# A two-block network on one core: more tokens by fetched rows in the first expert layer, fetches paced by eight, held lists, later modulation loads

## The chip, the cores and the metric

The kernel runs on one core of a Trainium2 chip. Its engines are TensorE (PE: matmuls and transposes), VectorE (DVE), ScalarE (ACT), GpSimd (POOL) and SyncE (SP), each with its own in-order queue of instructions; 16 DMA engines move data between HBM and the on-chip memory (SBUF). The metric is device time in microseconds of one execution. The kernel before took 2840.39 us, the median of three runs (2839.59 to 2842.22).

## The reference

A sequence of 256 tokens of width 1024, fp32, goes through two blocks. The part that matters here is the first block: two layers, each a mixer followed by an expert layer (`peer_ffn`); the mixer is an mLSTM in the first and a stick-breaking attention in the second. Before each half the input is normalised and modulated, `h * (1 + scale) + shift`, and after it gated; shift, scale and gate are six vectors of 1024 per layer, each the product of one conditioning vector with a 1024 x 1024 matrix (4 MB). The attention has two more such vectors for its shared keys and values.

```
def peer_ffn(h, w_q, sub_keys, peer_u, peer_v):   # per block of 128 tokens
    q = (xb @ w_q) as (128, 8 heads, 2, 128)
    s = q . sub_keys                              # (128, 8, 2, 128 keys)
    s_top, i_top = top_k(s, 16)
    cand = the 16 x 16 sums of both halves; g_top, pos = top_k(cand, 16)
    expert = 128 * i_first + i_second             # of 16384 experts
    act = gelu(u[expert] . xb);  out = sum softmax(g_top) * act * v[expert]
```

So each token uses 8 x 16 = 128 experts of 16384, and each expert has one row of 4 KB in a table u and one in a table v. The second block (two feed-forward pairs, an MLA and a forget-gate attention, a gated projection) is not touched.

## The kernel before

All stages run one after the other (`run`): mLSTM, expert layer 0 (`peer(0)`), attention (`stick`), expert layer 1 (`peer(1)`), then the second block. Weights stream through a ring of four 8 KB-per-partition tiles (`raw`, 1.05 MB each), loaded by SyncE's queue. A tool traces the program in order, places each engine's instructions by a simulated timeline, and may so move an instruction ahead of others of its engine; `issue_after(x)` forbids that it moves ahead of x on that engine.

**An expert layer does its tokens in two ways.** The first `TSL[l]` tokens (80 in layer 0, 96 in layer 1) are done by fetched rows: for one (token, expert) pair per partition, GpSimd's indirect DMA (`get`, L1392) fetches 128 rows of u (a 128x1024 tile), VectorE multiplies them with the token and sums (`up`, L1399), and later 128 rows of v are added, weighted, to an accumulator (`down`, L1416). That makes `TSL` fetches for u and as many for v. The other tokens are done densely: all 16384 experts' u against them (`u_phase`, L1443: 64 tiles of 1.05 MB, 16 matmuls each, with as many columns as there are dense tokens), gelu, times a matrix G of gates that is built from one-hot matrices (`g_phase`: VectorE builds them, 16 matmuls per 8 tokens, L1477), and times all of v (`v_phase`, L1494: 64 tiles).

**Order in an expert layer.** First the query projection `w_q`, with the scores and top-16 lists woven in. A list (`top16`, L1589 to L1593) is a maximum-of-8, a replacement, a second maximum-of-8 and two index searches on VectorE; each block of 128 tokens has 16 of them (`tops`), and then a routing step (`route`). Block 0 holds all tokens done by rows. Its lists and routing lead to `scatter`: expert numbers `ex` (L1335) and gates are spread over partitions by TensorE (L1343), masked and reduced on VectorE (L1347, L1349) into `sidx` and `sg`. The lists of block 1 only feed the one-hot matrices of dense tokens, but VectorE does them as soon as their scores exist. Then `par` weaves generators, in the order of the trace: twelve U tiles with the routing; twenty more with the rest of it, a part of the fetches `f` and of `extra`; 32 U tiles of the second group beside G of the first, 32 V tiles beside G of the second, 30 V tiles alone, each with a part of `f` and `extra`. The X tiles of the second U group lie in the memory that routing used. `extra` loads the modulation matrices that come next, a 128x1024 row tile at a time, by GpSimd's queue (`ada_acc`, L479): 48 tiles in layer 0, 8 in layer 1. They share six row buffers with the fetches (`row`).

**Pacing.** Every `PACE` fetches, `get` has TensorE transpose `PACE` columns of `sidx` (L1387), held behind the matmul traced last (`last_mm`), and ScalarE casts them to integers (`ix`, L1389, three buffers); GpSimd's fetches wait for that. So TensorE's position in its queue of tiles sets when a group of fetches may start.

**The attention's start.** `stick` normalises x, projects q (4 weight tiles), k and v (8), does 8 attention steps without weights, and the output projection (4). In `units`, after each weight tile once a credit is used up, one step of the modulation `ada` is taken: a 1.05 MB tile by SyncE's queue into the same ring, and two multiply-adds on VectorE (L497, L499). Eight such steps are taken there; they give shift and scale of the coming expert layer, used when `peer_open(1)` prepares its input after the attention steps. `bg_credit` starts at -2 * 2048, and each tile adds 2048.

Of the kernel before, what the change touches and what calls it, by code (L numbers as in the profile page):

```python
# [17 lines left out]
OP = mybir.AluOpType  # L18
AX = mybir.AxisListType
# [5 lines left out]
EPS = 1e-6  # L25
BIG = 1e30
GC = 64
TSL = (80, 96)
PACE = 4
GSC = 16384.0  # L30
QW = S + 2
TB = 8
# [65 lines left out]
def _units(l):  # L98

    return (0, 64), (64, TSL[l] - 64)  # L100

# [14 lines left out]
class Kern:  # L116
# [709 lines left out]
    def stick(self, ada):  # L826
        nc, I = self.nc, self.I
        m = self.mod[1]
        self.bg, self.bg_every, self.bg_credit = it.islice(ada, 8), 2048, -2 * 2048
        with self.tc.tile_pool(name="sky", bufs=1, reuse_waits="tile") as py, ExitStack() as inner:  # L830
            h2 = [py.tile([P, NK, S], F32R, name=f"hk{i}") for i in range(2)]
            pl = inner.enter_context(self.tc.tile_pool(name="sk", bufs=1, reuse_waits="tile"))
# [390 lines left out]
    def peer_open(self, l):  # L1223
# [4 lines left out]
        self.pr = self.pctx.enter_context(self.tc.tile_pool(name="pr", bufs=1, side="right", reuse_waits="tile"))  # L1228
        flat = self.pr.tile([P, GC * (S - TSL[l])], F32R, tag="X", name=f"late_{l}")
        n = NK * QW  # L1230
# [7 lines left out]
    def peer(self, l, extra=None):  # L1238


        nc, I = self.nc, self.I
        m = self.mod[l]
        TS, TD, UNITS = TSL[l], S - TSL[l], _units(l)
        NG = sum(n for _, n in UNITS)
        with ExitStack() as ctx:
# [12 lines left out]
            rp = rctx.enter_context(self.tc.tile_pool(name="rt", bufs=1, reuse_waits="tile"))  # L1258
            s_sb = [rp.tile([P, 16, P], F32, name=f"s_sb{i}_{l}") for i in range(2)]
# [38 lines left out]
            tv = [rp.tile([P, 16, 16], F32, name=f"tv{tb}_{l}") for tb in range(2)]  # L1298
            ti = [rp.tile([P, 16, 16], U32, name=f"ti{tb}_{l}") for tb in range(2)]
            ready = [], []  # L1300

            def tops(tb, n):
                for _ in range(min(n, len(ready[tb]))):
                    c = ready[tb].pop(0)
                    self.top16(rp, s_sb[tb][:, c, :], tv[tb][:, c, :], ti[tb][:, c, :])
            for c0 in range(0, 16, 4):
                pss = [self.ps("acc"), self.ps("acc")]
                for c in range(c0, c0 + 4):
                    hi, lo = next(us)
                    tops(0, 2)  # L1310
                    if c >= 2:
                        next(norm, None)
                    pq = self.ps()
                    self.lin_s(qT, hi, lo, P, pq[:, 0:QW])
                    qs = rp.tile([P, S], F32, tag="qs", bufs=2, name=f"qs_{l}_{c}")
                    sc = self.small(1, "qsh")
                    nc.scalar.copy(sc, pq[:, S:S + 1])
                    nc.vector.scalar_tensor_tensor(qs, rms, sc, pq[:, 0:S], OP.mult, OP.add)
                    for tb in range(2):
                        nc.tensor.matmul(pss[tb][:, (c - c0) * P:(c - c0 + 1) * P], qs[:, tb * P:(tb + 1) * P],  # L1320
                                         keys[:, c % 2, :], start=True, stop=True)
                for tb in range(2):
                    nc.scalar.activation(s_sb[tb][:, c0:c0 + 4, :], pss[tb].rearrange("p (a b) -> p a b", a=4), AF.Copy,
                                         scale=rs[tb])
                for r in ready:
                    r.extend(range(c0, c0 + 4))
# [4 lines left out]
            def scatter():  # L1331

                g, s0, s1 = chosen[0]
                e = rp.tile([P, P], F32, name=f"ex_{l}")
                nc.vector.scalar_tensor_tensor(e, s0, float(P), s1, OP.mult, OP.add)  # L1335
                if l:
                    nc.vector.tensor_scalar(e, e, float(l * P * P), None, OP.add)
                for i, (src, dst) in enumerate(((e, sidx), (g, sg))):
                    ps = self.ps()
                    o = 0  # L1340
                    for u, (t0, n) in enumerate(UNITS):
                        r = P // n
                        nc.tensor.matmul(ps[:, u * P:(u + 1) * P], spread[:, u, :], src, start=True, stop=True)  # L1343
                        tmp = rp.tile([P, P], F32, tag="r_sp", bufs=2, name=f"sp{i}{u}_{l}")
                        mk = smask[:, 0:r] if u == 0 else smask[:, 4:4 + r]
                        t3 = tmp.rearrange("p (k r) -> p k r", r=r)
                        nc.vector.tensor_mul(t3, ps[:, u * P:(u + 1) * P].rearrange("p (k r) -> p k r", r=r),  # L1347
                                             mk[:, None, :].to_broadcast([P, n, r]))
                        nc.vector.tensor_reduce(dst[:, o:o + n], t3, AX.X, OP.add)  # L1349
                        o += n  # L1350

            def route():
                while ready[0]:
                    tops(0, 2)
                    yield
                chosen[0] = yield from self.route(0, tv[0], ti[0], rp, pool)
                scatter()
                yield
                while ready[1]:
                    tops(1, 2)  # L1360
                    yield
                r1 = self.route(1, tv[1], ti[1], rp, pool)
                for _ in range(5):
                    next(r1)
                    yield
                self.routed(0, chosen[0], idx, TS)
                chosen[1] = yield from r1

            def fetched():
# [10 lines left out]
                def get(src, col):  # L1380

                    i = next(nth)
                    self.uid += 1
                    if i % PACE == 0:
                        ps = self.ps()
                        with self.tc.issue_after(self.last_mm.ins):
                            nc.tensor.matmul(ps[:, 0:PACE], self.ident, sidx[:, col:col + PACE], start=True, stop=True)  # L1387
                        held["ix"] = pool.tile([P, PACE], I32, tag="ix", bufs=3, name=f"ix_{self.uid}")
                        nc.scalar.copy(held["ix"], ps[:, 0:PACE])  # L1389
                    k = i % PACE  # L1390
                    row = self.row()
# [463 lines left out]
```

## Time and profile before

| what | value |
| --- | --- |
| median of 3 runs | 2840.39 us (2839.59 to 2842.22) |
| profiled execution | 2841.97 us |
| its span, first to last instruction | 2839.8 us |
| PE / PEld / DVE / ACT / POOL busy | 97 / 90 / 68 / 33 / 16% |
| mean granted TensorE clock | 0.986 |
| HBM read | 743.76 MB, 262 GB/s over the span |
| indirect fetches | 176 of u, 176 of v (80 + 96 each) |

How to read it: busy time is the union of an engine's instructions in the span; fp32 matmuls are recorded as two, so a dense tile of 16 matmuls shows as x32. DMA share is the mean busy share of 16 engines and can pass 1.0 where packets of two queues overlap. In the span, layer 0's first U matmul is at 238, its stage ends at about 907; layer 1's first is at 1125, and it ends at about 1745.

### The profile page before, as it was taken

To read this page: it belongs to the slowest core of one execution; us is meant where nothing else is said; L and a number is where in the kernel's file an instruction comes from. 1 tells how busy PE (TensorE), PEld (TensorE's weight loads), DVE (VectorE), ACT (ScalarE), POOL (GpSimd) and SP (SyncE) were. 2 spreads that over 40 slices of the span, in tenths; PEclk is the share of its full clock that TensorE was granted. 3 is DMA by queue.
4 is the path that set the end of the run, shared out by engine and by line. 5 is a ranking of instruction groups with operands and counts; after the bars stand their busy time and mean duration, and the time that the engine had idled before them with its cause. 6 is when DMAs were issued, how large, how long until landed. Compare 5 with 4: busy or idle time off the path is not lost.

```text
span 2839.8 us, 47705 instructions
## 1 busy us (share of the span) xinstructions
PE 2740.8 (97%) x19226; PEld 2544.7 (90%) x19226; DVE 1938.5 (68%) x4021; ACT 929.6 (33%) x1730; POOL 450.9 (16%) x445
## 2 busy tenths in 40 slices
PE   7999999999998999999999998999999999999999
PEld 4789989999998779999999987998799989877997
DVE  6778756767645978857777545667766666676665
ACT  4752111100000654111100002446654554456544
POOL 0000332333432000133344431000000000000000
PEclk9999999999999999999999999999999999999999
DMA  7655998999998634799999996554245555452553
GB/s 294 226 179 174 364 372 331 389 359 373 396 407 333 227 118 142 289 401 415 408 408 405 409 409 258 193 186 153 94 169 188 182 179 190 153 175 93 193 191 110
DMA packets 155580, 747.90 MB, mean 263 GB/s; under 512 B 15696, under 2 KB 17360, under 8 KB 111840
## 3 DMA queue, kind: packets, MB, share of 16 engines
q1 hardware_dynamic: 93984, 527.93, 49.9%
q0 software_dynamic: 58752, 213.94, 19.4%
q8 instruction: 151, 2.47, 0.4%
q10 hardware_dynamic: 2624, 3.00, 0.3%
q14 instruction: 69, 0.57, 0.1%
HBM read 743.76 MB, written 1.05 MB: 262 GB/s over the span
## 4 chain that ended last, share of the span: by engine, by line
PE 85%; DMA 7%; DVE 5%; ACT 2%; issue 1%; POOL 0%; SPq 0%; DVEq 0%; ACTq 0%; POOLq 0%
PE ps_acc L1494 17%; PE ps_mm L1443 17%; PE ps_mm L277 7%; PE ps_mm L279 7%; PE ps_mm L278 7%; DMA raw<-in_peer_v_dram 4%; PE ps_acc L244 4%; PE ps_acc L243 4%; PE ps_acc L245 4%; PE ps_acc L1149 3%; PE ps_acc L1151 3%; PE ps_acc L1150 3%; PE ps_mm L1477 1%; DMA raw<-in_ada_w_dram 1%; DVE wlo L229 1%
## 5 line engine op out<-in xcount | busy, mean ns | idle before, releaser
L229 DVE TENSOR_TENSOR wlo<-raw,whi 128x1024 fp32r<-128x1024 f32 (+1 forms) x440 | 532.6, 1214 | 243.4 <-ACT whi L228 232.7
L228 ACT CAST whi<-raw 128x1024 fp32r<-128x1024 f32 (+1 forms) x440 | 456.2, 1042 | 512.2 <-PE ps_mm L278 241.9
L1494 PE MATMUL ps_acc<-X,raw 128*128 128x176 f32 (+1 forms) x4096 | 608.0, 309 | 11.0 <-DMA raw<-in_peer_v_dram 10.8
L1443 PE MATMUL ps_mm<-hT,raw 128*128 128x176 f32 (+1 forms) x4096 | 604.6, 308 | 2.4 <-ACT jT L1673 2.4
L1494 PEld LDWEIGHTS ps_acc<-X,raw 128*128 128x128 f32 x4096 | 587.0, 191 | 16.2 <-DMA raw<-in_peer_v_dram 16.1
L1443 PEld LDWEIGHTS ps_mm<-hT,raw 128*128 128x128 f32 x4096 | 588.6, 191 | 3.4 <-ACT jT L1673 2.6
L277 PE MATMUL ps_mm<-xhi,whi 128*128 128x256 f32 (+1 forms) x1488 | 418.3, 283 | 7.4 <-ACT xhi L332 5.1
L278 PE MATMUL ps_mm<-xlo,whi 128*128 128x256 f32 (+1 forms) x1488 | 418.2, 282 | 3.3 <-DVE xlo L321 3.0
L279 PE MATMUL ps_mm<-xhi,wlo 128*128 128x256 f32 (+1 forms) x1488 | 417.9, 281 | 0.0
L1416 DVE SCALAR_TENSOR_TENSOR sacc<-row,dots,sacc 128x1024 f32<-128x1024 f32 x172 | 220.7, 1283 | 117.2 <-DMA row<-in_peer_v_dram,ix 116.2
L1399 DVE SCALAR_TENSOR_TENSOR row<-row,hn 128x1024 f32<-128x1024 f32 x176 | 213.1, 1224 | 114.7 <-DMA row<-in_peer_un_dram,ix 114.3
L277 PEld LDWEIGHTS ps_mm<-xhi,whi 128*128 128x128 f32 (+1 forms) x1488 | 279.6, 189 | 11.9 <-ACT xhi L332 5.3
L278 PEld LDWEIGHTS ps_mm<-xlo,whi 128*128 128x128 f32 (+1 forms) x1488 | 280.0, 188 | 7.3 <-DVE xlo L321 3.5
L279 PEld LDWEIGHTS ps_mm<-xhi,wlo 128*128 128x128 f32 (+1 forms) x1488 | 281.2, 189 | 0.5 <-DVE wlo L229 0.3
L1392 POOL DMA_INDIRECT row<-in_peer_un_dram,ix x176 | 209.9, 1192 | 446.7 <-ACT ix L1389 156.1
L1392 POOL DMA_INDIRECT row<-in_peer_v_dram,ix x176 | 197.2, 1120 | 340.2 <-ACT ix L1389 177.5
L1445 ACT ACTIVATE X<-ps_mm 128x352 f32<-128x352 f32 (+1 forms) x128 | 57.6, 450 | 495.5 <-PE ps_mm L1443 495.5
L1389 ACT CAST ix<-ps_mm 128x4 int32<-128x4 f32 x88 | 14.2, 161 | 511.8 <-PE ps_mm L1387 440.8
L1483 DVE SCALAR_TENSOR_TENSOR X<-ps_mm,X 128x128 f32<-128x128 f32 (+1 forms) x210 | 66.1, 365 | 125.2 <-PE ps_mm L1477 122.0
L1149 PE MATMUL ps_acc<-whi,ah 128*128 128x512 f32 x352 | 139.4, 396 | 0.0
L1151 PE MATMUL ps_acc<-whi,al 128*128 128x512 f32 x352 | 137.6, 392 | 0.0
L1150 PE MATMUL ps_acc<-wlo,ah 128*128 128x512 f32 x352 | 137.0, 389 | 0.0
(467 smaller groups left out, 3795.1 us busy)
## 6 DMA issues: line engine op xcount, KB each, us to landing
raw<-in_ffn_dram SPq DMA_DIRECT2D x132, 1024.0 KB, 4.8
raw<-in_peer_u_dram SPq DMA_DIRECT2D x128, 1024.0 KB, 7.9
raw<-in_peer_v_dram SPq DMA_DIRECT2D x128, 1024.0 KB, 11.3
raw<-in_ada_w_dram SPq DMA_DIRECT2D x28, 1024.0 KB, 5.4
row<-in_ada_w_dram POOLq DMA_DIRECT2D x40, 512.0 KB, 10.9
raw<-in_peer_wq_dram SPq DMA_DIRECT2D x16, 1024.0 KB, 4.8
raw<-in_fox_in_dram SPq DMA_DIRECT2D x12, 1024.0 KB, 5.1
raw<-in_ma_vo_dram SPq DMA_DIRECT2D x8, 1024.0 KB, 5.6
```

The costliest lines, as they stand in the source:

```text
L228: nc.scalar.copy(hi[:, 0:u], raw)
L229: nc.vector.tensor_sub(lo[:, 0:u], raw, hi[:, 0:u])
L277: nc.tensor.matmul(o, wh, xh[:, k, :], start=(k == 0), stop=False)
L278: nc.tensor.matmul(o, wh, xl[:, k, :], start=False, stop=False)
L279: self.last_mm = nc.tensor.matmul(o, wl, xh[:, k, :], start=False, stop=(k == NK - 1))
L1149: nc.tensor.matmul(o, ah[:, t], wh[:, n], start=(c == 0), stop=False)
L1150: nc.tensor.matmul(o, ah[:, t], wl[:, n], start=False, stop=False)
L1151: nc.tensor.matmul(o, al[:, t], wh[:, n], start=False, stop=(c == FFC - 1))
L1392: nc.gpsimd.indirect_dma_start(row, None, src, bass.IndirectOffsetOnAxis(held["ix"][:, k:k + 1], 0))
L1416: nc.vector.scalar_tensor_tensor(sacc[u], row, w, sacc[u], OP.mult, OP.add)
L1443: self.last_mm = nc.tensor.matmul(ps[:, i * TD:(i + 1) * TD], raw[:, o:o + P], hT[:, k, TS:S], start=(k == 0), stop=(k == NK - 1))
L1494: self.last_mm = nc.tensor.matmul(o, w, xs[:, 0, :], start=(first and c % 2 == 0), stop=last, skip_group_check=True)
```

## The change

The first layer does 96 tokens by rows (160 densely, 16 fewer), with two units of 64 and 32 tokens as the second layer has them. An index matmul and cast serve eight fetches. The top-16 lists of block 1 may not be placed ahead of the last reduction of `scatter`, in both layers. In the attention stage the first modulation step comes two weight tiles later.

```
-TSL = (80, 96)
-PACE = 4
+TSL = (96, 96)
+PACE = 8
@@ stick
-        self.bg, self.bg_every, self.bg_credit = it.islice(ada, 8), 2048, -2 * 2048
+        self.bg, self.bg_every, self.bg_credit = it.islice(ada, 8), 2048, -4 * 2048
@@ peer, tops(tb, n)
                 c = ready[tb].pop(0)
-                self.top16(rp, s_sb[tb][:, c, :], tv[tb][:, c, :], ti[tb][:, c, :])
+                with ExitStack() as hold:
+                    if tb:
+                        hold.enter_context(self.tc.issue_after(self.scattered.ins))
+                    self.top16(rp, s_sb[tb][:, c, :], tv[tb][:, c, :], ti[tb][:, c, :])
@@ peer, scatter()
-                        nc.vector.tensor_reduce(dst[:, o:o + n], t3, AX.X, OP.add)
+                        self.scattered = nc.vector.tensor_reduce(dst[:, o:o + n], t3, AX.X, OP.add)
```

## Rows read from the trace of the kernel before

**Rows 1.** The page's part 4: chain that ended last, shares by engine.

```profile
PE 85%; DMA 7%; DVE 5%; ACT 2%; issue 1%; POOL 0%; SPq 0%; DVEq 0%; ACTq 0%; POOLq 0%
```

**Rows 2.** Stretches of layer 0: window, length, engines' busy us, PEclk, DMA share, GB/s.

```profile
239.00:298.00 59.00, 59.00 (x400) 58.79 (x399) 54.05 (x283) 10.94 (x19) 0.00 (x0) 1.00 0.56 197
298.00:412.00 114.00, 108.42 (x716) 106.57 (x715) 68.29 (x127) 14.76 (x38) 46.04 (x43) 0.99 0.98 384
412.00:584.00 172.00, 167.80 (x1390) 166.64 (x1389) 119.64 (x196) 18.92 (x61) 54.60 (x56) 0.98 0.94 361
584.00:749.00 165.00, 165.00 (x1375) 162.83 (x1374) 117.71 (x243) 3.17 (x14) 59.99 (x56) 1.00 0.98 374
749.00:899.00 150.00, 150.00 (x1017) 149.86 (x1015) 72.08 (x78) 4.17 (x28) 61.10 (x63) 1.00 1.03 408
```

**Rows 3.** The same view, stretches of layer 1.

```profile
1125.00:1180.00 55.00, 55.00 (x410) 54.93 (x409) 51.81 (x262) 10.88 (x20) 0.00 (x0) 1.00 0.61 211
1180.00:1276.00 96.00, 93.61 (x681) 93.37 (x680) 60.31 (x145) 12.32 (x34) 38.59 (x35) 0.98 0.99 392
1276.00:1432.00 156.00, 156.00 (x1406) 155.27 (x1405) 116.24 (x188) 16.31 (x49) 61.38 (x57) 1.00 1.02 411
1432.00:1588.00 156.00, 156.00 (x1380) 154.73 (x1379) 114.38 (x238) 3.87 (x18) 70.06 (x59) 1.00 1.02 407
1588.00:1738.00 150.00, 139.20 (x973) 134.28 (x972) 68.72 (x73) 2.49 (x14) 52.41 (x51) 0.99 1.01 403
```

**Rows 4.** TensorE's timeline, both layers: start us, length us, instruction, count, idle before.

```profile
238.10 0.46 PE L1443 MATMUL ps_mm<-hT,raw 128*128 128x176 f32 x2
...
297.38 0.28 PE L1387 MATMUL ps_mm<-sidx,consts 128*128 128x4 f32 x2
...
311.93 0.28 PE L1387 MATMUL ps_mm<-sidx,consts 128*128 128x4 f32 x2
...
899.34 7.43 PE L1494 MATMUL ps_acc<-X,raw 128*128 128x176 f32 x48 [0.19 <-DMA raw<-in_peer_v_dram]
...
1125.09 0.43 PE L1443 MATMUL ps_mm<-hT,raw 128*128 128x160 f32 x2
...
1179.13 0.28 PE L1387 MATMUL ps_mm<-sidx,consts 128*128 128x4 f32 x2
...
1192.39 0.28 PE L1387 MATMUL ps_mm<-sidx,consts 128*128 128x4 f32 x2
```

**Rows 5.** GpSimd by line in layer 0: busy, mean ns, idle before by releaser.

```profile
L1392 POOL DMA_INDIRECT row<-in_peer_un_dram,ix x80 | 99.1, 1239 | 231.4 <-ACT ix L1389 104.4 <-DVE sg L1349 65.9 <-DVE row L1399 24.2
```

**Rows 6.** VectorE's timeline around the indices of layer 0, and routing's end in both.

```profile
278.04 0.29 DVE L1335 SCALAR_TENSOR_TENSOR ex<-r_sel,r_sel 128x128 f32<-128x128 f32 x1
...
284.54 0.09 DVE L1590 MATCH_VALUE_LOAD r_tmp<-tv,s_sb 128x8 f32 x1
...
285.66 0.09 DVE L1590 MATCH_VALUE_LOAD r_tmp<-tv,s_sb 128x8 f32 x1
...
289.60 0.27 DVE L1347 TENSOR_TENSOR sp<-ps_mm,smask 128x128 f32<-128x128 f32 x1
...
294.45 0.27 DVE L1349 TENSOR_REDUCE sidx<-sp 128x16 f32<-128x128 f32 x1
...
356.66 0.38 DVE L1656 TENSOR_TENSOR r_sel<-r_eq 128x128 f32<-128x128 f16 x1
...
1239.98 0.38 DVE L1656 TENSOR_TENSOR r_sel<-r_eq 128x128 f32<-128x128 f16 x1
```

**Rows 7.** VectorE's timeline at the attention stage's start.

```profile
913.30 0.75 DVE L497 TENSOR_SCALAR ada<-raw,cs 128x1024 f32<-128x1024 f32 x1 [1.87 <-DMA raw<-in_ada_w_dram]
...
914.57 1.28 DVE L499 SCALAR_TENSOR_TENSOR ada<-raw,cs,ada 128x1024 f32<-128x1024 f32 x1
```

**Rows 8.** TensorE's timeline at the last V weights of the attention stage.

```profile
988.09 1.39 PE L888 MATMUL ps_mm<-consts,k 128*128 128x128 f32 x8 [1.54 <-DVE k L859]
...
993.39 1.22 PE L243 MATMUL ps_acc<-whi,hk 128*128 128x512 f32 x2 [3.91 <-ACT whi L228]
```

## The prediction

> **What bounds the kernel now.** I read the chain of waits first, then the table of stages of the two expert layers, then the timelines of TensorE, VectorE and GpSimd at the places that the diff touches. The chain puts 85% of the span on TensorE and 7% on DMA [rows 1], but that mean hides two kinds of stage. In the first expert layer TensorE is busy in 150 of 150 us at the end and in 165 of 165 before it, while the DMA engines are also at 0.98 to 1.03 and move 361 to 408 GB/s [rows 2]. So this stage stands at two limits at once. In the second expert layer, which already sends 96 tokens by fetched rows, the DMA share is 1.01 to 1.02 at 403 to 411 GB/s in three of the four stretches after the fetches begin, and in its last stretch TensorE drops to 139 of 150 us [rows 3]: there the transfers bound it. That layer is thus a model, run in the same program, of what the first will be. Outside the expert layers the diff touches only the attention stage's start.
>
> **The first layer with 96 tokens.** A dense weight tile is 1.05 MB and 16 matmuls. Between two index matmuls three tiles pass in 311.93 - 297.38 = 14.55 us at 176 columns and 1192.39 - 1179.13 = 13.26 us at 160 [rows 4]: 4.85 against 4.42 us per tile, 0.43 less. Over 128 tiles TensorE is given 55 us, and four `g_phase` steps of 44 go too. Were TensorE alone the limit, that would be the gain.
>
> The bytes go the other way. 16 more tokens are 16 rows of 128 experts in each of two tables: 32 more fetches of a 128x1024 fp32 tile, 0.524 MB each, 16.8 MB. What the layer moves between its first fetch and its last dense tile is, from the stages, 114 x 384 + 172 x 361 + 165 x 374 + 150 x 408 = 228.8 MB in 601 us, 381 GB/s on average [rows 2]. It becomes 245.6 MB. (The dense bytes don't shrink: the same tiles multiply fewer columns.) The start moves: the first index matmul is held behind the matmul traced last, so it stands after twelve U tiles, at 297.38 for a stage that starts at 238.10, and at 1179.13 for 1125.09 in the other layer [rows 4]. With 12 x 0.43 = 5.2 us less, fetching starts near 292.8 instead of 298.
>
> So the question is the rate at which 245.6 MB move. The second layer moves 96 x 392 + 156 x 411 + 156 x 407 + 150 x 403 = 225.7 MB in 558 us: 404.5 GB/s; its saturated middle does 409 [rows 3]. The first layer's 361 to 384 before is a demand that TensorE set, since its last stretch reaches 408 as soon as there are no `g_phase` matmuls [rows 2]. Bounds: at 409 the bytes take 600 us and the last tile lands at 893, against 899 now [rows 4], 6 us earlier; at 395, half way between the old 381 and 409, they take 622 us and it lands at 915, 16 later. I take 406, near the second layer's row: 605 us, 898, 1.3 us earlier; with the last 1.5 tiles of matmuls 0.6 us shorter, **2 us gained**. Nearly all of the 55 us turns into waiting for tiles.
>
> The DMA page of the Trainium skill (DMA: Bandwidth & Descriptors, section Where 436 GB/s comes from) puts the limit of a transfer from HBM to SBUF at about 358 GB/s and the port ceiling at 435. By the first the layer would take an estimated 686 us and the change would cost 80 us; by the second an estimated 565 us, a gain of 40. The stages of this trace decide against the first: 407 and 411 GB/s were held for 156 us each [rows 3]. For the second see the last rival.
>
> **Fetches paced by eight.** Each index matmul, its psum tile, the cast on ScalarE and the GpSimd wait now serve eight fetches: the 40 + 48 groups of both layers become 24 + 24, and the matmul is 0.28 us [rows 4], so its own time is nothing beside the tiles. What may count is the gap: GpSimd waits 104 us for the index cast in the first layer's U rows alone [rows 5]. Two effects. A burst of eight keeps the row queue fed where it runs dry, above all just after the start: the second layer's first 96 us run at 392 instead of 409 GB/s [rows 3], worth 96 x 17 / 409 = 4 us. Against it, only six row buffers exist, so the last two of a burst wait for VectorE to free one, and then nothing is asked for until the next burst. No row shows bursts of eight; the bounds are all of the 4 us and a loss of the same size, and I take **2 us gained** in the second layer (in the first it is in the 406). The queue behind the waiting GpSimd instruction holds the later rows and the modulation rows of `ada_acc`, nothing of the dense tiles, which SyncE issues.
>
> **The held lists.** In the first layer VectorE has the expert numbers at 278.04 and masks the spread result only at 289.60; between them it does the second block's lists, one per 1.12 us (284.54, 285.66) [rows 6]. The indices are there at 294.45 + 0.27 = 294.7. That is 2.7 us ahead of the index matmul now, but 1.9 us behind its new place at 292.8: without the hold TensorE would wait, with it the indices come some 10 us sooner and it doesn't. So the hold protects the 5 us above and adds none; in the second layer the index matmul is tied to the twelfth tile and does not move: nothing. Its price is VectorE work put later: sixteen lists, of 1.12 us and about 0.46 us for the first search and index (two of 0.28, overlapping), 25 us, now start near 283 and end near 308, where the second block's candidates began right behind the mask at 289.60 [rows 6]. The routing of that block ended at 357.0 and 1240.4 [rows 6], so it moves to about 375 and 1258. Who waits: the second U group, whose X tiles reuse that memory, near 405 and at 1276 [rows 3]. The margin is 30 and 18 us, so I cost it at nothing; if it is used up the stall is paid by TensorE, and in part hidden by the transfers that bound the stage.
>
> **Modulation later.** The attention stage loads eight 1 MB modulation tiles in the weight ring of four, one after each weight tile from the third on; now from the fifth. At the stage's start one such tile stands in VectorE's queue ahead of the last residual adds: a wait of 1.87 us, an operation to 914.05, and a second one of 1.28 us at 914.57 that delays the remaining adds [rows 7]. Without them those adds start when their psum tile is ready; of 1.87 + 0.67 + 1.2 us I count 3. In the projections two more modulation tiles are still ahead of the last V weights, where TensorE waits 1.54 + 3.91 us [rows 8]; one of the eight now falls behind them, so I count 1 of these 5.5. The work that moves into attention (four or five VectorE operations of 1.28 us, and the transposes of the two sums) lies under that loop, where VectorE is not full. Bounds: 8.5 us gained; 3 us lost, if the moved operations land in front of an attention step. I take **4 us gained**.
>
> **Sum.** 2 + 2 + 4 = 8 us. The profiled execution took 2841.97 us, 2.2 more than its span of 2839.8, and stands 1.6 above the median of the runs, 2840.39. The sum is made against the profiled execution (2834.0) and, as a difference, put on the median: **2832 us**.
>
> **Rivals.**
> - *All of it shows:* 409 GB/s from the start, the whole ramp, all waits of the attention stage: 6 + 0.6 + 6 + 8.5 = 21 us, 2819. For it: 407 to 411 held over 312 us in the second layer [rows 3]. Against: every stage of rows 2 and 3 has a start and an end below that.
> - *The rows eat more than TensorE gives back (slower):* the first layer has 47 modulation rows beside its fetches, which the second layer hardly has, in the same six buffers, and TensorE stands in order behind the sums of those rows. If rows and tiles then don't keep the queues full and the rate stays at 395, the layer ends 15 us later; with the other 6 us gained 2850. It decides against the change from 245.6 / 0.403 = 609 us on, that is below 403 GB/s. For it: the second layer as a whole, without those rows, has only 404.5. Against: the last stretch, with such rows, does 408 [rows 2].
> - *The ends don't pay:* rate 404, no ramp gain, the attention stage bound by its weight tiles anyway: 2840.
> - *The second block comes late:* its lists run at half speed between rows, 25 us more: 1283 against 1276, 7 us in the second layer, which leaves 2839.
> - *The rate isn't capped at 409:* TensorE stays the limit and pays 55 us: 2787. For it: TensorE was busy throughout in rows 2. Against: the second layer, with the lighter matmuls, doesn't pass 411. (The 435 GB/s of the page above would lie between.)
>
> **How the numbers follow.** Forecast 0.42 (its own range 2826 to 2838), all of it 0.10, slower rival 0.21, ends don't pay 0.17, late lists 0.06, no cap 0.04. About 0.2%, 5.7 us, can be told from no change. Of the forecast's 0.42 some 0.34 lie beyond it: faster 0.34 + 0.10 + 0.04 = 0.48; same 0.08 + 0.17 + 0.06 = 0.31; slower 0.21. The range reaches from the full gain to the slower rival, 2817 to 2851, which leaves out the uncapped case and the far half of the slower one.
>
> **What would show it.** Right: U and V matmuls of the first layer at 4.4 us per tile between waits, but a DMA share over 1.0 and 403 to 409 GB/s from the first fetch on, TensorE waiting for tiles there, and the last tile landing within 10 us of 899; first fetch near 293, and unchanged at 1180 counted from its stage's start; no modulation operation of VectorE ahead of the residual adds. Wrong: a first layer shorter by 20 us or more (the rate was no cap), rates of 380 in it with TensorE idle (the row queue starves), or a TensorE gap where the second U group begins (the lists).

## The result and the profile after

The changed kernel takes 2878.6 us (median; 2874.8 to 2885.9), the kernel before 2841.3 us on the same chip: a ratio of 1.0135, 95% interval 1.0122 to 1.0148. It is 38 us slower; I had forecast 8 us faster, with 2851 as the upper end. The profiled execution after took 2885.9 us (span 2884.1).

Its span is 44.3 us longer than that of before. By stages: the mLSTM +8.5 (its clock, in the last section, not the change), the first expert layer +40.1 (673.9 to 714.0, first U tile to last `back` matmul, which spreads the fetched rows' sums), attention -6.6 (213.1 to 206.6, from there to the second layer's first U tile), second expert layer +3.1 (615.9 to 619.0, first U tile to last V tile), the rest of the span -0.8. So nearly all of the change's loss is in the first expert layer.

TensorE's waits there, by line waited for: total us, times, longest. Before:

```profile
PE ps_mm L548 <- DVE ada L546: 5.6, 1, 5.6
PE ps_mm L517 <- DVE ada L483: 4.2, 1, 4.2
PE ps_acc L1494 <- DMA raw<-in_peer_v_dram: 0.2, 1, 0.2
```

After:

```profile
PE ps_mm L517 <- DVE ada L483: 35.5, 3, 12.7
PE ps_mm L548 <- DVE ada L546: 22.3, 1, 22.3
PE ps_mm L1534 <- DVE sacc L1419: 17.9, 1, 17.9
PE ps_acc L1497 <- DMA raw<-in_peer_v_dram: 11.5, 24, 2.5
PE ps_mm L1446 <- ACT jT L1676: 5.6, 1, 5.6
```

TensorE waits for weight tiles for only 11.5 us, where I had expected nearly 55. It waits 57.8 us for modulation sums (L517 transposes one, L548 spreads one over the partitions), 45.1 of them while weight tiles are left and 12.7 behind the last one; 17.9 us for the last fetched rows; and 5.6 us for a result of the routing (`jT`). Its timeline, answering [rows 4]:

```profile
300.09 0.28 PE L1390 MATMUL ps_mm<-sidx,consts 128*128 128x8 f32 x2
...
383.24 3.75 PE L548 MATMUL ps_mm<-ada,consts 128*128 128x512 f32 x4 [22.33 <-DVE ada L546]
...
468.01 1.94 PE L517 MATMUL ps_mm<-consts,ada 128*128 128x128 f32 x8 [11.72 <-DVE ada L483]
...
583.15 1.94 PE L517 MATMUL ps_mm<-consts,ada 128*128 128x128 f32 x8 [11.12 <-DVE ada L483]
...
910.54 8.46 PE L1497 MATMUL ps_acc<-X,raw 128*128 128x160 f32 x48 [2.52 <-DMA raw<-in_peer_v_dram]
931.65 1.94 PE L517 MATMUL ps_mm<-consts,ada 128*128 128x128 f32 x8 [12.66 <-DVE ada L483]
...
953.24 2.07 PE L1534 MATMUL ps_mm<-sacc,back 128*128 128x512 f32 x2 [17.86 <-DVE sacc L1419]
```

The dense weights end at 919; the last row's product comes 34 us later. The stages, answering [rows 2]:

```profile
247.00:301.00 54.00, 54.00 (x403) 54.00 (x402) 34.60 (x153) 10.73 (x19) 0.00 (x0) 1.00 0.60 215
301.00:361.00 60.00, 54.33 (x388) 53.85 (x386) 49.65 (x207) 5.95 (x15) 19.80 (x22) 0.94 0.99 396
361.00:383.00 22.00, 0.00 (x0) 0.00 (x0) 21.69 (x49) 2.58 (x5) 9.54 (x7) 0.59 0.63 210
383.00:405.00 22.00, 21.76 (x132) 19.73 (x133) 14.82 (x25) 2.54 (x6) 7.26 (x9) 0.87 0.80 277
405.00:604.00 199.00, 176.16 (x1506) 175.24 (x1506) 133.63 (x205) 19.43 (x63) 71.53 (x74) 0.94 0.96 379
604.00:760.00 156.00, 155.47 (x1377) 153.37 (x1376) 114.85 (x242) 2.99 (x11) 62.01 (x59) 1.00 1.02 407
760.00:919.00 159.00, 148.01 (x1036) 142.25 (x1034) 71.23 (x80) 2.62 (x16) 49.86 (x56) 0.99 1.02 406
919.00:953.00 34.00, 3.72 (x12) 2.53 (x12) 28.36 (x25) 1.63 (x10) 24.83 (x25) 0.58 0.85 319
```

From 301 to 953 length times rate sums to 248.8 MB in 652 us, 382 GB/s. In the two stretches where tiles and rows both flow it is 406 and 407, over 315 us: the rate that I assumed exists. The Trainium skill (DMA: Bandwidth & Descriptors, Where 436 GB/s comes from) puts the limit of such transfers at about 358 GB/s; these two stretches stand above it. The rate is lost elsewhere: 210 and 277 GB/s for 44 us around L548, 379 in the stretch with the next two sums, 319 at the end, where the rows are nearly alone (8.9 of 10.9 MB; the rest are the attention stage's first weights). At L548 the fall is in the wait itself. At the next sum it comes behind the wait: during it the ring fills up (1.3 MB of tiles beside 3.5 MB of rows), and the 24 us that follow are slow:

```profile
456.30:468.00 11.70, 0.00 (x0) 0.02 (x1) 10.33 (x14) 0.00 (x0) 6.00 (x7) 0.68 1.00 405
468.00:480.00 12.00, 11.99 (x80) 11.96 (x81) 8.93 (x12) 1.58 (x9) 3.16 (x4) 0.75 0.86 284
480.00:492.00 12.00, 12.00 (x115) 11.92 (x113) 6.63 (x12) 1.48 (x4) 4.24 (x4) 1.00 0.77 271
```

From 361 to 383 TensorE does nothing while VectorE is busy 21.7 of 22 us: it is VectorE that is late there. VectorE, answering [rows 6]:

```profile
281.83 0.29 DVE L1338 SCALAR_TENSOR_TENSOR ex<-r_sel,r_sel 128x128 f32<-128x128 f32 x1
290.93 0.29 DVE L1350 TENSOR_TENSOR sp<-ps_mm,smask 128x128 f32<-128x128 f32 x1 [8.80 <-PE ps_mm L1346]
...
294.36 0.49 DVE L1350 TENSOR_TENSOR sp<-ps_mm,smask 128x128 f32<-128x128 f32 x2 [2.82 <-PE ps_mm L1346]
...
297.85 0.29 DVE L1350 TENSOR_TENSOR sp<-ps_mm,smask 128x128 f32<-128x128 f32 x1 [2.61 <-PE ps_mm L1346]
...
298.38 1.64 DVE L1592 MAX8 tv<-s_sb 128x8 f32<-128x128 f32 x8
...
382.42 1.27 DVE L546 TENSOR_TENSOR ada<-ada,adab 1x512 f32<-1x512 f32 x2
...
387.27 0.40 DVE L1659 TENSOR_TENSOR r_sel<-r_eq 128x128 f32<-128x128 f16 x1
```

The hold makes VectorE idle 8.8 + 2.8 + 2.6 = 14.2 us for three TensorE results, with the second block's lists ready to be done; they begin at 298.4, when the rows begin to come, and routing ends 141 us after the stage's first U tile instead of 119 (387.3 less 246.6; 356.7 less 238.1 before). The sum for L548 (382.42) comes just ahead of that end.

### The profile page after: what moved, and what is told of

Read it like the earlier page. It is cut to its first block, busy times and chain, and to the rows that moved or that the text cites. A ratio compares the mean times of both kernels' runs of the same rounds, so it can differ in the third digit from the quotient of the medians.

```text
span 2884.1 us, 47449 instructions
## 1 busy us (share of the span) xinstructions
PE 2701.1 (94%) x19082; PEld 2492.6 (86%) x19082; DVE 1968.6 (68%) x4044; ACT 922.5 (32%) x1691; POOL 471.9 (16%) x477
## 4 chain that ended last, share of the span: by engine, by line
PE 71%; DMA 17%; DVE 7%; issue 3%; ACT 2%; POOL 1%; ACTq 0%; DVEq 0%; POOLq 0%; SPq 0%
PE ps_acc L1497 13%; PE ps_mm L1446 9%; DMA raw<-in_peer_v_dram 8%; PE ps_mm L277 7%; PE ps_mm L279 7%; PE ps_mm L278 7%; PE ps_acc L244 4%; PE ps_acc L243 4%; PE ps_acc L245 4%; DMA row<-in_peer_un_dram,ix 4%; DMA row<-in_peer_v_dram,ix 3%; PE ps_acc L1149 3%; PE ps_acc L1151 3%; PE ps_acc L1150 3%; DMA row<-in_ada_w_dram 2%
## 5 line engine op out<-in xcount | busy, mean ns | idle before, releaser
L1497 PE MATMUL ps_acc<-X,raw 128*128 128x160 f32 x4096 | 582.5, 302 | 23.5 <-DMA raw<-in_peer_v_dram 23.4
L1497 PEld LDWEIGHTS ps_acc<-X,raw 128*128 128x128 f32 x4096 | 560.8, 190 | 35.5 <-DMA raw<-in_peer_v_dram 34.5
L1446 PE MATMUL ps_mm<-hT,raw 128*128 128x160 f32 x4096 | 579.8, 303 | 8.0 <-ACT jT L1676 6.8
L1446 PEld LDWEIGHTS ps_mm<-hT,raw 128*128 128x128 f32 x4096 | 566.9, 192 | 9.6 <-ACT jT L1676 7.3
L1419 DVE SCALAR_TENSOR_TENSOR sacc<-row,dots,sacc 128x1024 f32<-128x1024 f32 x188 | 241.1, 1283 | 128.4 <-DMA row<-in_peer_v_dram,ix 127.0
L1402 DVE SCALAR_TENSOR_TENSOR row<-row,hn 128x1024 f32<-128x1024 f32 x192 | 232.4, 1222 | 117.6 <-DMA row<-in_peer_un_dram,ix 117.5
L1395 POOL DMA_INDIRECT row<-in_peer_un_dram,ix x192 | 216.9, 1130 | 455.9 <-DVE tv L1592 121.7
L1395 POOL DMA_INDIRECT row<-in_peer_v_dram,ix x192 | 211.2, 1100 | 318.5 <-DVE sacc L1419 137.7
L1448 ACT ACTIVATE X<-ps_mm 128x320 f32<-128x320 f32 x128 | 55.5, 438 | 440.0 <-PE ps_mm L1446 439.9
L1392 ACT CAST ix<-ps_mm 128x8 int32<-128x8 f32 x48 | 7.9, 167 | 379.7 <-PE ps_mm L1390 314.6
```

Of the source, the lines that this page charges most:

```text
L1395: nc.gpsimd.indirect_dma_start(row, None, src, bass.IndirectOffsetOnAxis(held["ix"][:, k:k + 1], 0))
L1402: nc.vector.scalar_tensor_tensor(row, row, 1.0, hnat[:, u, :], OP.mult, OP.mult, accum_out=dots[:, col:col + 1])
L1419: nc.vector.scalar_tensor_tensor(sacc[u], row, w, sacc[u], OP.mult, OP.add)
L1446: self.last_mm = nc.tensor.matmul(ps[:, i * TD:(i + 1) * TD], raw[:, o:o + P], hT[:, k, TS:S], start=(k == 0), stop=(k == NK - 1))
L1497: self.last_mm = nc.tensor.matmul(o, w, xs[:, 0, :], start=(first and c % 2 == 0), stop=last, skip_group_check=True)
```

## The experiments

Stage lengths are from each profiled execution: first layer, attention, second layer as above (before 673.9, 213.1, 615.9; after 714.0, 206.6, 619.0); times are medians; the ratio, with its 95% interval, is to the kernel before on the same chip.

**Undoing one part.** Four kernels, each the changed one with one edit back.

```
e1_no_hold:  if tb:  ->  if False:        (lists not held)
e2_tsl80:    TSL = (96, 96)  ->  (80, 96)
e3_pace4:    PACE = 8  ->  4
e4_bg2:      -4 * 2048  ->  -2 * 2048      (attention's modulation)
```

> The changed kernel with the hold alone undone: the second block's lists start again behind the candidates; 96 tokens, pacing by eight and the later modulation stay. Theory A (the hold puts 25 us of lists and the routing behind them among the row work, VectorE becomes the late engine from 300 to 430, TensorE then waits in order for the ada sums and the transfers fall to 215 to 239 GB/s for 40 us): most of the loss goes, 2845 to 2850. Theory B (the 32 extra fetches beside 47 modulation rows through six row buffers make the rows lag the dense tiles): it stays at 2865 to 2875, with the last rows still some 30 us behind the last V tile. Theory C (pacing by eight lets TensorE run ahead of the rows): also near 2870. Index matmul of layer 0 about 7 us later than with the hold under all three.

Measured 2863.2 us, 1.0086 (1.0069 to 1.0103); first layer 702.1. The time lies between the theories and is nearer B: the hold is worth 12 us of the layer, 28 stay, and the last row ends 36 us behind the last V tile. Its index matmul came 54.05 us after the first U tile, against 53.5 with the hold, not 7 us later. TensorE's waits:

```profile
PE ps_mm L517 <- DVE ada L483: 37.5, 3, 14.0
PE ps_mm L1534 <- DVE sacc L1419: 17.7, 1, 17.7
PE ps_acc L1497 <- DMA raw<-in_peer_v_dram: 12.2, 25, 2.5
PE ps_mm L548 <- DVE ada L546: 10.2, 1, 10.2
```

Only L548 is clearly shorter, 10.2 instead of 22.3: the hold works mainly through that one sum.

> The changed kernel with the first layer back at 80 tokens; hold, pacing by eight and later modulation stay. Theory A: the hold still collides with the row work, so 2850 to 2860. Theory B: the loss goes, 2835 to 2842, the last row of layer 0 finishes within a few us of the last V tile. Theory C: it stays above 2855, since the pacing is the same in both layers.

Measured 2845.8 us, 1.0016 (1.0003 to 1.0028); first layer 681.0, 33 us under the changed kernel. The time lies 4 us above theory B's range and 4 below A's; the last row again ends before the last V tile, as B says. The wait at L548 is still 17.2 us, at L517 3.4.

> The changed kernel with pacing by four instead of eight. Theories A and B: within 6 us of the changed kernel, 2870 to 2882, and the gap between the last V tile and the last row product in layer 0 stays near 30 us. Theory C: TensorE is held back to the rows, the stretch in which it has nothing left but rows (919 to 953 us) shrinks to under 10 us, 2845 to 2855.

Measured 2881.0 us, 1.0141 (1.0124 to 1.0158). Theory C falls: the stretch with rows alone stays (926 to 961, 34 us as in the changed kernel), and the first layer is 10 us longer in this execution (724.2; the medians differ by 2).

> The changed kernel with the attention stage's modulation started after the second weight tile again, as before. Under all theories of the expert layer the loss there stays. If the later start gains what I put on it, this kernel is 2 to 4 us slower than the changed one, 2880 to 2883; if the start never mattered, the same within 1 us; the stretch from the attention stage's first projection to its output weights goes from 117 back to 118.6 us.

Measured 2879.2 us, 1.0140 (1.0123 to 1.0157): the total can't tell. The attention stage takes 209.6 us with the early start, 3.0 more.

**Is it the modulation rows?** In two kernels seven of the eight rows of each modulation vector are left out; the places of the sums stay. One has 96 tokens (on e1), one 80 (on before).

```
             for k in range(NK if self.slack else 0):
-                r = self.row(); nc.gpsimd.dma_start(r, ...); sum it
+                if k == 0: (the same)
```

> The changed kernel without the hold (96 tokens, pacing by eight, later modulation), and with only the first of the eight 128x1024 modulation rows of each vector fetched and summed in the expert layers: the modulation is incomplete, the places of its sums in TensorE's order are the same. Some 42 fetches, 22 MB, go. Theory B (96 tokens fail because the 47 modulation rows share the row queue and TensorE stands in order behind their sums): no more waits at the sums, layer 0 bound by TensorE's 545 us of matmuls, 2780 to 2795, that is 40 to 55 us under the same cut with 80 tokens. Rival (the 32 expert rows alone are too much for the row queue, or VectorE's lists delay everything anyway): not below the same cut with 80 tokens, 2825 or more.

> The kernel before with the same modulation rows left out (one of eight is fetched and summed in the expert layers). Its layer 0 is bound by TensorE, so all theories say little: the 10 us of waits at the two sums and a little at the end go, 2828 to 2838. It is the reference for the cut with 96 tokens.

Measured 2769.0 us (0.9734, 0.9719 to 0.9749) and 2821.5 us (0.9932, 0.9910 to 0.9954): without those rows the kernel with 96 tokens is 52 us faster, of which 41 are in the first layer (618.8 against 659.8) and 4.5 in the attention stage, which has its later start in the first of the two alone. Both lie below what I had expected, by 11 and 7 us. The layer with 96 tokens, stretches as in [rows 2]:

```profile
292.00:400.00 108.00, 107.66 (x799) 106.44 (x798) 69.14 (x174) 15.41 (x38) 42.14 (x41) 1.00 1.00 407
400.00:560.00 160.00, 160.00 (x1460) 159.19 (x1460) 121.08 (x214) 16.64 (x55) 61.24 (x56) 1.00 1.01 405
560.00:700.00 140.00, 140.00 (x1222) 138.76 (x1222) 99.10 (x200) 2.59 (x10) 58.89 (x53) 1.00 1.02 402
700.00:850.00 150.00, 138.56 (x969) 132.84 (x968) 69.41 (x77) 3.92 (x24) 49.53 (x50) 0.99 1.01 399
```

Here 399 to 407 GB/s, 403 on average, hold from the first fetch on, and TensorE is busy in 546 of 558 us. The 32 expert rows are not too many for the row queue; they and the 47 modulation rows together are. The cut takes VectorE's 42 sums of 1.28 us away too, but VectorE is not what holds the rows back for most of the layer: in e1 from 405 to 896 us it stands idle 130 of 491 us for rows that haven't landed. Around L548 it is busy.

**The bytes of those rows, or TensorE's place behind their sums?** All rows are fetched, but the transposes and broadcasts stand three steps later in the order.

```
         acc = yield from self.ada_acc(src, self.cs)
-        if self.slack:
+        for _ in range(4 if self.slack else 0):
             yield
```

with `ne` 14 to 18 (3 to 4) and `islice(a1, 27)` to 36, so that the rows keep their places.

> The changed kernel without the hold, all rows fetched, but the transposes and broadcasts that finish a modulation vector stand three steps later in the order (four steps behind its last row instead of one; 18 steps of modulation in each third of a layer instead of 14, so that the rows keep their density). Theory B1 (the loss is TensorE standing idle in order behind a sum, 13, 13, 10 and 11 us, while the dense queue is full): those waits shrink to under 5 us each, 2840 to 2850. Theory B2 (the row queue is simply behind the tiles by then, and a wait taken away comes back at the end of the layer): 2858 to 2868, with the last V tile earlier and a longer stretch with rows alone behind it.

Measured 2847.2 us, 1.0012 (1.0000 to 1.0024), 16 us under e1; first layer 685.3. The time is B1's: of TensorE's waits at sums, 47.7 us in e1 (14.0 of them behind the last tile), two rows are left,

```profile
PE ps_mm L517 <- DVE ada L483: 28.3, 2, 27.8
...
PE ps_mm L548 <- DVE ada L546: 1.3, 2, 1.1
```

and the 27.8 us lie behind the last tile, where TensorE has nothing else to do. But the rows are not done by then. V ends at 869, the last row's product at 916:

```profile
405.00:560.00 155.00, 152.09 (x1336) 150.86 (x1335) 118.25 (x186) 15.37 (x47) 64.80 (x59) 0.99 1.02 410
560.00:700.00 140.00, 137.68 (x1241) 135.00 (x1240) 108.95 (x227) 3.87 (x18) 52.10 (x53) 1.00 1.03 408
700.00:869.00 169.00, 157.51 (x1107) 151.99 (x1105) 75.53 (x96) 2.89 (x17) 55.74 (x61) 0.99 1.02 405
869.00:899.00 30.00, 2.17 (x11) 1.96 (x11) 26.25 (x23) 0.49 (x2) 20.00 (x19) 0.56 0.97 359
899.00:918.00 19.00, 3.53 (x7) 1.32 (x6) 15.33 (x14) 1.15 (x8) 12.36 (x17) 0.59 0.72 265
```

So part of what is gained at the sums comes back as rows alone at the end (47 us instead of 36), as B2 said. The layer moves 248.8 MB in 627 us, 397 GB/s; at 406 it would be 613. Whether the waits at the sums are what 96 tokens lose against 80 this run can't tell by itself: that takes the late sums with 80 tokens too (`g1_late_80`, below).

> The changed kernel, hold and all, with the sums of the modulation vectors three steps later in the order, as in the run without the hold. If the hold costs through TensorE's wait behind the first sum (22 us with it, 10 without), it costs little here: 2848 to 2854, within 6 us of that run's 2847. If it costs by the work that it puts off (VectorE and the rows), its 12 us stay: 2857 to 2863.

The same on the changed kernel, with its hold: 2851.3 us, 1.0023 (1.0011 to 1.0034); first layer 691.6. The late sums take 27 us off it, and the hold costs 4 instead of 15: what it puts off hurts mainly through the first sum (L548 9.5 us here).

**One part alone on the kernel before.**

> The kernel before with the hold alone (80 tokens, pacing by four, early modulation). My prediction's term: nothing, 2840 to 2843. Theory A', after the first calls: the lists and the second block's routing are put between the row work, the first sum that TensorE stands behind (5.6 us before) comes 10 to 12 us later, so 5 to 12 us slower in layer 0 and nothing in layer 1, 2846 to 2854.

Measured 2850.4 us, 1.0023 (1.0013 to 1.0033): the hold alone costs 7 us, 10.6 in the first layer, where L548 waits 13.1 us instead of 5.6.

> The kernel before with pacing by eight alone. My prediction's term: 2 us faster in the second layer, nothing apart from that, 2839 to 2842. By the layers so far: the second layer from its first U tile to its last V tile took 618 to 619 us with eight and 615 to 616 with four, so about 3 us slower there, and nothing in the first layer with 80 tokens, 2844 to 2847.

Measured 2839.4 us, 0.9986 (0.9977 to 0.9996): about 4 us faster, the sign of my term. But the second layer, where I had put it, is no shorter (616.7); over all runs it takes 613 to 617 us with four and 614 to 619 with eight (f1 and f2, with rows left out, aside). In its one profiled execution the first layer is 2.5 us shorter (671.4) and attention 1.5; where the 4 us come from stays open.

> The kernel before with the later start of the attention stage's modulation alone. By my term 4 us faster, 2837 (bounds 8.5 faster, 3 slower); by the last call, where the stage took 146 to 147 us from the expert layer's end to the output weights with the late start, 149.4 with the early one and 153.4 in the kernel before, 3 to 7 us faster, 2834 to 2838.

Measured 2837.4 us, 0.9977 (0.9963 to 0.9991): 6 us faster, the attention stage 206.5 instead of 213.1. The three small parts don't add up: alone they give +7, -4 and -6, together with 80 tokens (e2) +5. That difference stays open.

**A version that beats both.** If TensorE's place behind the sums costs this much, it costs something in the kernel before too: `g1_late_80` is e8 with the late sums.

> The kernel before (80 tokens, pacing by four, no hold) with the later modulation of the attention stage and the sums of the modulation vectors three steps later in the order. The stage's 6 us stay; the two waits of TensorE behind sums in the first layer, 5.9 and 4.2 us in the run with the late modulation alone, go: 10 us more, 2827 to 2829 where the other gave 2837. If those waits only come back elsewhere (transfers bind the last 150 us of that layer), 2835 to 2838.

Measured 2818.4 us, 0.9921 (0.9908 to 0.9935): 22 us under before by the ratio (25 by the medians, 2843.6 on this chip), 60 under the changed kernel, from five lines, and 9 under what I had expected. First layer 659.3; no wait at any sum. It gains 14.6 us on e8 in the layer where 10.1 us of waits went (9.8 in before). A wait has an aftermath: two stretches of before, right behind its two waits, and the first of them here:

```profile
361.00:372.00 11.00, 10.26 (x52) 8.50 (x53) 8.83 (x15) 1.75 (x4) 6.08 (x5) 0.84 0.90 315
445.00:457.00 12.00, 11.96 (x67) 11.99 (x68) 6.91 (x7) 1.61 (x9) 3.98 (x3) 0.80 0.80 274
```

```profile
361.00:372.00 11.00, 11.00 (x70) 10.19 (x68) 6.11 (x12) 2.18 (x5) 7.94 (x6) 1.00 0.89 306
```

A clock of 0.84 and 0.80 over 23 us is an estimated 11 x 0.16 + 12 x 0.20 = 4.2 us more; with the waits that is 14.3.

This run is also the control for f3. The late sums gain 16.8 us of the first layer with 96 tokens (e1 to f3) and 14.6 with 80 (e8 to g1). So 96 tokens (here always with pacing by eight) cost 28.1 us of the layer with the sums early (702.1 against 673.9) and still 25.9 with them late (685.3 against 659.3): the waits at the sums burden both kernels nearly alike and explain some 2 of the 28 us. The rest is the rows' queue, which now ends last. With the sums late V ends 22 us sooner with 96 tokens than with 80 (631.9 against 654.1 us after the first U tile), but 13.7 of the rows' 125.3 MB are left by then, and the rest of the layer takes 53 us instead of 5.

## Why the prediction was wrong

- **Fetch start, right.** 54.7 us after the stage's start predicted, 53.5 measured (54.0 without the hold).
- **Bytes, right for the layer.** 248.8 MB moved instead of 245.6. The rows are as counted (125.3 MB after, 108.5 before, 16.8 more). The tiles' queue moved 122.7 MB instead of 119.4, because the attention stage's first weights, issued from 900 us on, land before the last rows do.
- **The rate, the step that failed.** "I take 406, near the second layer's row" and "nearly all of the 55 us turns into waiting for tiles". At 406 the bytes would need 613 us; they needed 652, at 382. The chip gives 406 when tiles and rows both flow. I treated them as one stream of bytes, but they are two queues, and each has its own end. The 39 us part by the runs: 11 are the hold's (641 us in e1), 14 the sums' (627 in f3), 14 are left, 10 of them in the last 49 us of f3, where 15.8 MB move at 322 GB/s with the rows nearly alone. The second layer was no model: it has 8 modulation rows, the first 47; with the rows cut, the first layer does run at the second's rate (f1).
- **What the sums do.** The sums tie the two queues, because TensorE, in its order, stands behind them. With lighter tiles it comes to a sum sooner, with more rows the sum comes later: the first one was reached 118.1 us after the first U tile and ready at 123.6 in before, reached at 115.1 and ready at 125.3 in e1; the second 202.7 and 206.9, then 197.8 and 211.0. Before pays such waits too, and that is why they are part of the gap to my 406, but little of the loss against 80 tokens; that loss is the rows that are left when the tiles are done.
- **What I could have seen.** [rows 2] have TensorE at 108.4 of 114 and 167.8 of 172 us. These 9.8 us were the two waits at sums; I wrote that TensorE was busy throughout and read the rates of 361 to 384 as a mere demand. They were a demand too: f2, where the rows are cut, runs at 342 to 362 with TensorE busy throughout:

```profile
412.00:584.00 172.00, 172.00 (x1442) 170.84 (x1439) 110.41 (x192) 18.28 (x61) 46.35 (x47) 1.00 0.92 342
...
749.00:892.00 143.00, 143.00 (x971) 143.00 (x970) 54.08 (x58) 4.53 (x28) 48.64 (x50) 1.00 0.95 362
```

- **The right rival, priced too low.** "The rows eat more" named the modulation rows and the sums. Its price came from 395, half way up from 381, for which no row spoke; at 381 my own 245.6 MB take 645 us, 40 later than my 605, 2872. That should have been its price and the range's end. Its mechanism too is half of it: it has TensorE behind the sums, not the rows that go on alone behind the last tile.
- **The hold, 0 predicted, 12 of the 40 us.** Two errors. It was to protect 5 us; it protected 0.5. I kept the indices at 294.7, but they come off matmuls that stand between the U tiles, and move with them: without the hold they were there at 288.3, 2.4 us before the index matmul (290.64). And I asked only who waits for the end of routing (U group 2, which had margin), not who else is queued on VectorE from 298 to 387: the rows, and with them the sum of L548.
- **Pacing, near in size, not in place.** 2 predicted, 4 measured alone, nothing clear in company (e3). I had put it in the second layer, which is no shorter: as far as the runs show, the size is luck.
- **Attention, right.** 4 predicted within a bound of 8.5; 6.6 by the stage, 6 by medians alone. From the last `back` matmul to the first key projection 34.9 us became 29.6, where I had counted 3 us; no modulation operation stands among the residual adds any more [rows 7]. The waits of [rows 8] are both gone, but from there to the next layer's query projection the stage is only 1.8 us shorter (1 counted).

What stays argued is why the rows get no larger share before the tiles end: six row buffers, pacing and the equal shares of the last section all bear on it, and of these only the pacing was changed by itself.

## What to carry to other kernels

Before counting bytes against a rate, list the places where one engine's order ties two queues together, and see which side reaches them first once the work per step changes: the waits of 4 to 6 us in the profile of before were worth 15 us. Moving such a consumer a few steps behind its producer gained 15 to 17 us of the layer in both kernels. Then count each queue's bytes to its own end: with 96 tokens the tiles were done and the rows went on for 34 to 47 us. An operation that is put off costs whoever is queued behind it, not only whoever needs its result.

## What the runs showed of the hardware

- TensorE came out of the long wait at half speed. The four matmuls of L548 took 3.75 us behind the wait of 22 us (granted clock 0.59 in the 22 us before) and 1.88 us in `g1_late_80`, where TensorE had not stopped: the levels of 1.2 and 2.4 GHz.
- The mLSTM, which is the same code in all, has a stretch whose clock differs from run to run. Before and after:

```profile
100.00:125.00 25.00, 25.00 (x122) 19.65 (x121) 15.59 (x37) 17.76 (x45) 0.00 (x0) 0.93 0.53 180
```

```profile
100.00:125.00 25.00, 25.00 (x86) 18.73 (x86) 9.77 (x17) 12.59 (x35) 0.00 (x0) 0.59 0.39 135
```

The first expert layer began at 238.1 and 246.6 us in these two, at 236.6 to 246.2 over the other profiled runs, without regard to the edit. That is up to 10 us of scatter in single executions, which is why stages are compared above.

- Tiles and rows share the transfers evenly while both have work. The queues of e1 from 850 to 882 us (packets, MB, share of the engines; the first carries the tiles, the second the rows):

```profile
q1 hardware_dynamic: 1740, 6.70, 52.5%
q0 software_dynamic: 1741, 6.34, 49.9%
```

As many packets of one as of the other. The Trainium skill (DMA: Bandwidth & Descriptors, Queues, rings and completion order) says that each DMA engine goes round its queues packet by packet; the trace's shares agree, 1740 to 1741, though it does not show the single turns. So here the rows, once behind, did not catch up while the tiles had work: 9.1 MB of them were left when V ended at 896.
